# Weight sums of a Strassen-style MLP made during the input projection, silu by tanh, and other buffers for the output projection

## The chip, the cores and the metric

One core of a Trainium2 chip runs the kernel. The metric is the time of one execution on the device in microseconds (us): the median of three runs of the kernel before is 2321.2 us (2319.56 to 2322.18).

The engines are TensorE (PE; its weight loads are listed as PEld), VectorE (DVE), ScalarE (ACT), GpSimd (POOL) and SyncE (SP). Nearly all DMAs of this kernel are issued on SP, a few on POOL. Each engine works through its own list of instructions in order, and an instruction that waits holds up what is behind it in that list.

## The reference

One layer of a streaming encoder over 2048 prompt frames and 64 sample frames, model width 1024, all in float32:

```
a = rmsnorm(x, norm1)
qa, ka, va, qr, kr, vr, gr = split(a @ w_in)      # queries and keys are rotated by position
attn = windowed attention with a sink per head (window of 2 chunks of 64 frames + the own chunk)
ret  = chunkwise retention with a state per head
r    = ret * rsqrt(mean(ret * ret) + EPS) * silu(gr)
h    = x + concat(attn, r) @ w_out
u    = relu(rmsnorm(h, norm2) @ w_up)             # 1024 -> 4096
y    = h + (u * u) @ w_down                       # 4096 -> 1024
out  = rmsnorm(y, norm_f)                         # and new keys, values and retention states
```

Here silu(g) = g / (1 + exp(-g)), which is also 0.5 * g * (1 + tanh(g / 2)). In the kernel g = rs * z, where z is the product before the norm and rs the norm's factor of a row.

## The kernel before

The 2112 tokens are worked in 16 tiles of 128 and one of 64 in the projection, and in NP = 3 parts of PN = 704 columns (two blocks of NB = 352) after it. A product in full precision is made of three matmuls: each operand is split into a high part (ACT, L620) and a low part (DVE, L621), and high x high, high x low and low x high are added up in PSUM.

**The input projection** (0 to about 750 us) goes through the tiles twice: phase `ph` = 0 and 1 each have half of the heads' columns, in three column groups `ci` (384, 512 and 512 columns). `groups` (L549) lists (phase, tile, column group). The loop at L570 starts, at the first group of a tile, the loads of the next tile: `xr` (the input, 512 KB), `rt` (rotation tables) and, in phase 0, `xk` (the input again, for the norm). Then `group` (L516) issues the matmuls of a group and, among them, what `run_ready` finds due of the attention and retention work of earlier tiles. The order of PE and SP in this stage is that order of the code (`manual_schedule`, L553); DVE, ACT and POOL are ordered by the framework's scheduler. The gate `sig` is made of ACT's exp (L352), DVE's add (L353), DVE's reciprocal (L354) and one more DVE operation (L356). `xl`, the low part of the input, is a subtraction on POOL (L154). `hl` (L232) holds the split rotated queries and keys, `pl` (L315) the low part of the transposed softmax weights.

The weights of this stage pass through the pool `wraw` (4 buffers, tag "raw"); it is used for weights at the start of a phase only.

**The output projection** (about 750 to 945 us) is `out_part` (L671): for each part and each of 8 column tiles `d` it loads and splits weights `wo` (L676 to L681) and multiplies with `mhl`, the split mixture, which `load_mix` (L660) loads through `mraw` (3 buffers of its own). `hooks` names the work issued after step d of a part: `norm_part` (L704: two matmuls with ones per block, names `pn` and `nr`, then DVE operations on `nt`), `a_sums` (L713, sums of the activation) and `a_operand` (L728, loading and splitting such a sum to `ah` and `al`).

**The MLP** multiplies blocks of matrices with seven products in place of eight (`ORDER`, `RIGHT`, `LEFT`). Each weight block needs four sums of its quarters: `left_sums` (L650), three on DVE and one on POOL. For the up weights this happens in part 0 (`up_weights`, L778): load two blocks of 512 KB (`up`), make the sums (`su`), use them, and store them to `uscr`; parts 1 and 2 load them from there (`upr`, 256 KB each). `up_pair` (L799) makes one pair of column blocks; there are 16 pairs in a part. For the down weights, `down_sums` (L765) loads two blocks of 512 KB (`dnraw`), makes the sums (`sd`) and stores them to `sscr`, once after every second pair of parts 1 and 2. All these loads go to the 6 buffers of `rawslot` (pool `wr`). From about 1644 us the down projection reads `sscr` (`dr`, split to `wd`), and its matmuls are L971 to L973.

After the input projection its pools are given back (`p1.close()`, L592), and the pools of the later stages lie over the same memory; a buffer laid over an earlier one waits until that one's last user has finished. `side="right"` puts a pool at the other end of the memory.

## Time and profile before

| | |
|---|---|
| median of 3 runs | 2321.2 us (2319.56 to 2322.18) |
| the profiled execution, its own time | 2321.18 us |
| its span in the trace | 2319.4 us |
| PE busy | 97% of the span |
| DVE / ACT / POOL busy | 70% / 48% / 20% |
| memory read / written | 348.28 MB / 135.99 MB |

The page lists busy time of each engine, the granted TensorE clock, DMA queues, the chain of work that ended last, and groups of instructions. A row of a group reads: line, engine, operation, output <- inputs, partitions x elements, count | busy us, mean ns of one | idle time of the engine just before them and what ended it. A row of the timeline reads: start, duration (both us), engine, line, operation, and in brackets the idle time before it and what ended it. A row of stretches reads: from:to and length in us, then busy time and count of PE, PEld, DVE, ACT and POOL, the granted clock (1.00 is full), the mean busy share of the 16 DMA engines (the records of transfers can overlap, so it can come out above 1) and GB/s. A row of DMA issues reads: destination <- source, issuing queue, kind, count, KB each, median us from issue to landing.

In the chain that ended last, PE has 42% of the span, DMA 8% and DVE 6%; the costliest lines are the down projection's L971 to L973.

### The profile page before, as it was taken

To read this page: it belongs to the slowest core of one execution; us is meant where nothing else is said; L and a number is where in the kernel's file an instruction comes from. 1 tells how busy PE (TensorE), PEld (TensorE's weight loads), DVE (VectorE), ACT (ScalarE), POOL (GpSimd) and SP (SyncE) were. 2 spreads that over 40 slices of the span, in tenths; PEclk is the share of its full clock that TensorE was granted. 3 is DMA by queue.
4 is the path that set the end of the run, shared out by engine and by line. 5 is a ranking of instruction groups with operands and counts; after the bars stand their busy time and mean duration, and the time that the engine had idled before them with its cause. 6 is when DMAs were issued, how large, how long until landed. Compare 5 with 4: busy or idle time off the path is not lost.

```text
span 2319.4 us, 35611 instructions
## 1 busy us (share of the span) xinstructions
PE 2243.5 (97%) x13256; PEld 2134.9 (92%) x13256; DVE 1634.6 (70%) x2645; ACT 1109.3 (48%) x1985; POOL 462.9 (20%) x533
## 2 busy tenths in 40 slices
PE   7999999999998999799999999999999999999998
PEld 5888888888886999799999899999999999999998
DVE  6676677666666567887787778777766876677665
ACT  5444454444434433355565556655554444444452
POOL 5444343433333111211000000000000200110012
PEclk9999999999998999899999999999999999999999
DMA  6222223111114778776699999999976776677662
GB/s 191 78 66 70 79 91 116 56 49 47 43 53 143 243 245 288 272 245 232 233 318 345 356 321 334 335 320 302 368 242 235 270 272 243 225 266 275 233 211 78
DMA packets 242734, 486.55 MB, mean 210 GB/s; under 512 B 20560, under 2 KB 126224, under 8 KB 242560
## 3 DMA queue, kind: packets, MB, share of 16 engines
q1 hardware_dynamic: 238592, 474.40, 60.4%
q0 software_dynamic: 3968, 9.87, 1.4%
q8 instruction: 104, 1.70, 0.3%
q14 instruction: 70, 0.57, 0.1%
HBM read 348.28 MB, written 135.99 MB: 209 GB/s over the span
## 4 chain that ended last, share of the span: by engine, by line
PE 42%; DMA 8%; DVE 6%; issue 2%; ACT 1%; SPq 0%; DVEq 0%; POOL 0%; ACTq 0%
PE y L971 10%; PE y L973 9%; PE y L972 9%; DMA up<-in_wup 3%; DMA upr<-uscr 2%; PE b L811 2%; PE b L813 2%; PE b L812 2%; DVE wu L621 2%; PE a L811 1%; PE a L813 1%; PE c L811 1%; PE a L812 1%; PE c L813 1%; PE c L812 1%
## 5 line engine op out<-in xcount | busy, mean ns | idle before, releaser
L973 PE MATMUL y<-vh,wd 128*128 128x352 f32 x1344 | 438.1, 326 | 2.1 <-DVE wd L621 2.1
L971 PE MATMUL y<-vh,wd 128*128 128x352 f32 x1344 | 439.2, 327 | 0.6 <-ACT wd L620 0.6
L972 PE MATMUL y<-vl,wd 128*128 128x352 f32 x1344 | 434.2, 323 | 0.0
L529 PE MATMUL z<-w,xh 128*128 128x512 f32 (+1 forms) x816 | 326.1, 400 | 7.3 <-ACT w L86 7.3
L530 PE MATMUL z<-w,xh 128*128 128x512 f32 (+1 forms) x816 | 310.2, 380 | 1.3 <-DVE w L87 1.3
L620 ACT ACTIVATE wd<-dr 128x1024 fp32r<-128x1024 f32 x168 | 177.2, 1056 | 268.2 <-PE y L973 184.4
L532 PE MATMUL z<-w,xl 128*128 128x512 f32 (+1 forms) x768 | 288.9, 376 | 0.1
L621 DVE TENSOR_TENSOR wd<-dr,wd 128x1024 fp32r<-128x1024 f32 x168 | 208.5, 1244 | 113.3 <-ACT wd L620 110.9
L971 PEld LDWEIGHTS y<-vh,wd 128*128 128x128 f32 x1344 | 253.6, 189 | 0.9 <-ACT wd L620 0.9
L973 PEld LDWEIGHTS y<-vh,wd 128*128 128x128 f32 x1344 | 252.0, 187 | 2.4 <-DVE wd L621 2.4
L972 PEld LDWEIGHTS y<-vl,wd 128*128 128x128 f32 x1344 | 253.1, 188 | 0.0
L811 PE MATMUL b<-ah,wu 128*128 128x352 f32 x576 | 188.2, 328 | 7.9 <-DVE u L822 6.6
L922 POOL TENSOR_TENSOR acc<-acc,sq 128x352 f32<-128x352 f32 x41 | 68.9, 1681 | 605.3 <-ACT sq L918 605.3
L813 PE MATMUL b<-ah,wu 128*128 128x352 f32 x576 | 186.5, 324 | 0.0
L812 PE MATMUL b<-al,wu 128*128 128x352 f32 x576 | 185.9, 323 | 0.0
L529 PEld LDWEIGHTS z<-w,xh 128*128 128x128 f32 x816 | 156.2, 191 | 25.8 <-ACT w L86 7.7
L530 PEld LDWEIGHTS z<-w,xh 128*128 128x128 f32 x816 | 156.2, 191 | 23.0 <-DVE w L87 5.2
L620 ACT ACTIVATE wu<-upr 128x512 fp32r<-128x512 f32 x224 | 134.5, 625 | 88.6 <-DMA upr<-in_wup 53.0
L621 DVE TENSOR_TENSOR wu<-upr,wu 128x512 fp32r<-128x512 f32 x224 | 151.4, 698 | 34.2 <-ACT wu L620 33.4
L532 PEld LDWEIGHTS z<-w,xl 128*128 128x128 f32 x768 | 144.8, 189 | 23.5 <-DVE xl L154 0.4
L621 DVE TENSOR_TENSOR vl<-rv,vh 128x1408 fp32r<-128x1408 f32 x84 | 137.3, 1638 | 36.7 <-ACT vh L620 35.6
L620 ACT ACTIVATE vh<-rv 128x1408 fp32r<-128x1408 f32 x84 | 115.8, 1379 | 48.2 <-DMA rv<-vscr 28.8
(292 smaller groups left out, 5108.4 us busy)
## 6 DMA issues: line engine op xcount, KB each, us to landing
rv<-vscr SPq DMA_DIRECT2D x84, 704.0 KB, 5.7
vscr<-C SPq DMA_DIRECT2D x48, 1056.0 KB, 7.4
dr<-sscr SPq DMA_DIRECT2D x96, 512.0 KB, 4.5
dr<-in_wdn SPq DMA_DIRECT2D x72, 512.0 KB, 4.8
upr<-uscr SPq DMA_DIRECT2D x128, 256.0 KB, 6.7
upr<-in_wup SPq DMA_DIRECT2D x96, 256.0 KB, 6.5
up<-in_wup SPq DMA_DIRECT2D x32, 512.0 KB, 6.0
uscr<-su SPq DMA_DIRECT2D x32, 512.0 KB, 2.9
```

What stands on the lines that cost most here:

```text
L529: nc.tensor.matmul(z[:, :n], xh[:, k], wh, start=k == 0, stop=False)
L530: nc.tensor.matmul(z[:, :n], xh[:, k], wl, start=False, stop=k == NK - 1 and xl is None)
L532: nc.tensor.matmul(z[:, :n], xl[:, k], wh, start=False, stop=k == NK - 1)
L620: nc.scalar.activation(h, x, AF.Copy)
L621: sub(l, x, h.bitcast(F32))
L811: nc.tensor.matmul(o, wh, ah[:, k], start=k == 0 and i in (1, 6, 5), stop=False, skip_group_check=True)
L812: nc.tensor.matmul(o, wh, al[:, k], start=False, stop=False, skip_group_check=True)
L813: nc.tensor.matmul(o, wl, ah[:, k], start=False, stop=k == 3 and i in (2, 4, 3), skip_group_check=True)
L922: nc.gpsimd.tensor_add(self.acc, self.acc, sq)
L971: nc.tensor.matmul(o, wh, vh, start=f == 0, stop=False)
L972: nc.tensor.matmul(o, wh, vl, start=False, stop=False)
L973: nc.tensor.matmul(o, wl, vh, start=False, stop=f == 15)
```

## The change

It has four parts, all in one diff.

1. **Sums.** `sum_unit(u)` makes 64 units, 32 of the up weights and 32 of the down weights. A unit loads two pieces of 256 KB into a buffer `sr`, makes four sums of 128x256 on DVE into `st`, and stores 512 KB to `uscr` or `sscr`. Both buffers come from `wraw`. The projection's loop first stores the unit of the group before, then loads the next one, then starts the tile's own loads. Units run from tile 3 of phase 0 until the weights of phase 1 come, and from the third tile of phase 1 on. `left_sums` and `down_sums` are gone, and part 0 of the up projection loads its seven operands from `uscr` and `wup`, as parts 1 and 2 do.
2. **Gate.** ACT computes tanh(z * rs / 2) in place of the exp; DVE's add and reciprocal are gone; `sig` becomes (tanh + 1) * z. The missing factor rs / 2 goes into the row factor `rr` of the retention output, by way of `ss`, for one more small POOL operation a tile in phase 0.
3. **Pools.** `wr`, `wp` and `wd` go to the right side and `qp` to the left, so that `qp` (the mixture's buffers) lies over `wraw` and the input's first weights. `mraw` is taken from the six `rawslot` buffers, not from three of its own.
4. **Hooks.** `norm_part(0)` and `norm_part(1)` come one step d later, `norm_part(2)` after the second pair of the up projection, not the first.

```
@@ -68,7 +68,7 @@
...
-    nrsc = cp.tile([128, NT], F32, name="nrsc")
+    hrs = cp.tile([128, NT], F32, name="hrs")
...
@@ -165,7 +165,8 @@
             ms = xp.tile([128, 1], F32, name="ms")
             nc.gpsimd.tensor_scalar(ms[:T], ss[:T, t:t + 1], 1.0 / D, EPS, op0=ALU.mult, op1=ALU.add)
             nc.gpsimd.tensor_tensor(rs[:T, t:t + 1], ms[:T], mhalf[:T, 0:1], op=ALU.pow)
-            nc.gpsimd.tensor_scalar(nrsc[:T, t:t + 1], rs[:T, t:t + 1], -1.0, None, op0=ALU.mult)
+            nc.gpsimd.tensor_scalar(hrs[:T, t:t + 1], rs[:T, t:t + 1], 0.5, None, op0=ALU.mult)
+            nc.gpsimd.tensor_scalar(ss[:T, t:t + 1], ms[:T], 4.0 / 128, None, op0=ALU.mult)
...
@@ -347,13 +348,12 @@
...
+
...
         sig = wk.tile([128, 256], F32, name="sig")
-        nc.scalar.activation(sig[:T], gz, AF.Exp, scale=nrsc[:T, t:t + 1])
-        nc.vector.tensor_scalar(sig[:T], sig[:T], 1.0, None, op0=ALU.add)
-        nc.vector.reciprocal(sig[:T], sig[:T])
+        nc.scalar.activation(sig[:T], gz, AF.Tanh, scale=hrs[:T, t:t + 1])
         c.sil = sig
-        nc.vector.scalar_tensor_tensor(sig[:T], gz, rs[:T, t:t + 1], sig[:T], op0=ALU.mult, op1=ALU.mult)
+        nc.vector.scalar_tensor_tensor(sig[:T], sig[:T], 1.0, gz, op0=ALU.add, op1=ALU.mult)
...
@@ -391,7 +391,7 @@
...
-        nc.gpsimd.tensor_scalar(s2[:T], s2[:T], 1.0 / 128, EPS, op0=ALU.mult, op1=ALU.add)
+        nc.gpsimd.tensor_scalar(s2[:T], s2[:T], 128 * EPS, ss[:T, t:t + 1], op0=ALU.add, op1=ALU.mult)
         nc.gpsimd.tensor_tensor(rr[:T], s2[:T], mhalf[:T], op=ALU.pow)
...
@@ -567,7 +567,38 @@
...
+    def sum_unit(u):
+
+
+        w, j, h = u // 32, u % 32 // 2, u % 2
+        r, s = (wraw.tile([128, 4, 256], F32, name=n, tag="raw") for n in ("sr", "st"))
+        if w == 0:
+            c = slice(h * 256, h * 256 + 256)
+            src = [wup[e].rearrange("p (a c) -> p a c", a=2)[:, :, c] for e in (j, j + 16)]
+            dst = uscr[:, j, :, c]
+        else:
+            d, c = j // 4, slice((j % 4 * 2 + h) * 256, (j % 4 * 2 + h) * 256 + 256)
+            src = [wdn[e].rearrange("p (a f) n -> p a (f n)", a=2)[:, :, c] for e in (d, d + 4)]
+            dst = sscr[:, d, :, c]
+        for k in range(2):
+            nc.sync.dma_start(r[:, 2 * k:2 * k + 2], src[k])
+        L11, L12, L21, L22 = (r[:, k] for k in range(4))
+        nc.vector.tensor_add(s[:, 0], L21, L22)
+        nc.vector.tensor_sub(s[:, 2], L11, L21)
+        nc.vector.tensor_sub(s[:, 1], s[:, 0], L11)
+        nc.vector.tensor_sub(s[:, 3], L12, s[:, 1])
+        return lambda: nc.sync.dma_start(dst.rearrange("s p c -> p s c"), s)
+
+    todo = list(range(64))
+    store = None
+    first, change = groups.index((0, 3, 0)), groups.index((0, S - 2, 0))
+
     for i, (ph, t, ci) in enumerate(groups):
+        if store:
+            store()
+            store = None
+        if todo and (first <= i < change or ph == 1 and t > 1):
+            store = sum_unit(todo.pop(0))
...
@@ -585,6 +616,7 @@
...
+    assert not todo and not store
...
@@ -595,11 +627,11 @@
...
-    wr = ctx.enter_context(pool(name="wr", bufs=6))
+    qp = ctx.enter_context(pool(name="qp", bufs=16))
     ar = ctx.enter_context(pool(name="ar", bufs=2))
-    qp = ctx.enter_context(pool(name="qp", bufs=16, side="right"))
+    wr = ctx.enter_context(pool(name="wr", bufs=6, side="right"))
     upper = ExitStack()
-    wp = upper.enter_context(pool(name="wp", bufs=9))
+    wp = upper.enter_context(pool(name="wp", bufs=9, side="right"))
...
@@ -647,13 +679,6 @@
...
-    def left_sums(sA, sB, L11, L12, L21, L22):
-
-        add(sA[:, 0], L21, L22)
-        nc.gpsimd.tensor_sub(sB[:, 0], L11, L21)
-        sub(sA[:, 1], sA[:, 0], L11)
-        sub(sB[:, 1], L12, sA[:, 1])
-
...
@@ -661,7 +686,7 @@
...
         for f in range(8):
-            raw = op.tile([128, PN], F32, name="mraw", bufs=3)
+            raw = rawslot("mraw")[:, :PN]
             nc.sync.dma_start(raw, mscr[f, :, n0:n0 + PN])
             t = qp.tile([128, 2, PN], F32R, name="mhl", tag="q")
             split(t[:, 0], t[:, 1], raw)
@@ -748,12 +773,11 @@
...
         accs[0] = out_part(0, mixes[0], {})
         accs[1] = out_part(1, mixes[1], {
-            0: [lambda: norm_part(0, accs[0])],
+            1: [lambda: norm_part(0, accs[0])],
             2: [later(a_sums, 0, 0, opslot), lambda: put(mixes, 2, load_mix, 2)],
             3: [later(a_sums, 0, 1, opslot)], 4: [later(a_sums, 0, 2, opslot)], 5: [later(a_sums, 0, 3, opslot)]})
         accs[2] = out_part(2, mixes[2], {
-            0: [lambda: norm_part(1, accs[1])],
-            1: [lambda: put(A, (0, ORDER[0]), a_operand, 0, ORDER[0])],
+            1: [lambda: norm_part(1, accs[1]), lambda: put(A, (0, ORDER[0]), a_operand, 0, ORDER[0])],
             2: [lambda: put(A, (0, ORDER[1]), a_operand, 0, ORDER[1]), later(a_sums, 1, 0, opslot)],
             3: [lambda: put(A, (0, ORDER[2]), a_operand, 0, ORDER[2]), later(a_sums, 1, 1, opslot)],
             4: [lambda: put(A, (0, ORDER[3]), a_operand, 0, ORDER[3]), later(a_sums, 1, 2, opslot)],
@@ -762,30 +786,7 @@
...
-    def down_sums(u):
-        d, fq = u // 4, u % 4
-        c = slice(fq * 512, fq * 512 + 512)
-        rw = []
-        for e in (d, d + 4):
-            r = rawslot("dnraw").rearrange("p (a n) -> p a n", a=2)
-            nc.sync.dma_start(r, wdn[e].rearrange("p (a f) n -> p a (f n)", a=2)[:, :, c])
-            rw.append(r)
-        sA, sB = (rawslot("sd").rearrange("p (a n) -> p a n", a=2) for _ in range(2))
-        left_sums(sA, sB, rw[0][:, 0], rw[0][:, 1], rw[1][:, 0], rw[1][:, 1])
-        nc.sync.dma_start(sscr[0:2, d, :, c].rearrange("a p n -> p a n"), sA)
-        nc.sync.dma_start(sscr[2:4, d, :, c].rearrange("a p n -> p a n"), sB)
-
-    def up_weights(p, j):
-        if p == 0:
-            r0, r1 = rawslot("up0"), rawslot("up1")
-            nc.sync.dma_start(r0, wup[j])
-            nc.sync.dma_start(r1, wup[j + 16])
-            L11, L12, L21, L22 = r0[:, :512], r0[:, 512:], r1[:, :512], r1[:, 512:]
-            sA, sB = (rawslot("su").rearrange("p (a n) -> p a n", a=2) for _ in range(2))
-            left_sums(sA, sB, L11, L12, L21, L22)
-            nc.sync.dma_start(uscr[0:2, j].rearrange("a p n -> p a n"), sA)
-            nc.sync.dma_start(uscr[2:4, j].rearrange("a p n -> p a n"), sB)
-            return {1: L11, 6: sA[:, 1], 5: sA[:, 0], 7: sB[:, 0], 2: L12, 4: L22, 3: sB[:, 1]}
+    def up_weights(j):
         src = {}
         for n, i in enumerate(ORDER):
             if n % 2 == 0:
@@ -797,7 +798,7 @@
...
     def up_pair(p, j, after):
-        src = up_weights(p, j)
+        src = up_weights(j)
         a, b, c = psum("a"), psum("b"), zp.tile([128, 512], F32, name="c", tag="z")
         bank = {1: a, 2: a, 6: b, 7: b, 4: b, 5: c, 3: c}
         C = up.tile([128, 8, NB], F32, name="C", bufs=2)
@@ -842,16 +843,14 @@
...
             for j in range(16):
                 up_pair(p, j, after)
-                if (p, j) == (0, 0):
+                if (p, j) == (0, 1):
                     norm_part(2, accs[2])
                 if p == 1 and j in (2, 4, 6, 8):
                     a_sums(2, j // 2 - 1, arslot)
-                if p > 0 and j % 2:
-                    down_sums(8 * (p - 1) + j // 2)
     upper.close()
-    wd = ctx.enter_context(pool(name="wd", bufs=4))
+    wd = ctx.enter_context(pool(name="wd", bufs=4, side="right"))
     xp2 = ctx.enter_context(pool(name="xp2", bufs=1, side="right"))
...
```

On SP, in the input projection in phase 0, where one tile's DMAs are issued (`xr`, `rt`, `xk` as above). Before, these three rows are a whole tile:

```order
L142 DMA xr<-in_xt 128x8x128
L160 DMA rt<-in_rot 128x384
L163 DMA xk<-in_xtok 128x1024
L142 DMA xr<-in_xt 128x8x128
L160 DMA rt<-in_rot 128x384
```

And after the change (`sr` is a unit's load, `st` its sums):

```order
L142 DMA xr<-in_xt 128x8x128
L160 DMA rt<-in_rot 128x384
L163 DMA xk<-in_xtok 128x1024
L590 DMA uscr<-st 128x4x256
L584 DMA sr<-in_wup 128x2x256 x2
L590 DMA uscr<-st 128x4x256
L584 DMA sr<-in_wup 128x2x256 x2
L590 DMA uscr<-st 128x4x256
L584 DMA sr<-in_wup 128x2x256 x2
L142 DMA xr<-in_xt 128x8x128
```

Three units stand between the loads of two tiles, and each store, which waits for its sums, stands ahead of the next unit's loads.

On DVE, in the input projection, from the softmax weights `p` of a tile to the queries and keys `hl`, before:

```order
L300 TENSOR_SCALAR p<-p,sm 128x192 x4
L376 TENSOR_TENSOR sd<-pss,dm 128x256
L353 TENSOR_SCALAR sig<-sig 128x256
L354 RECIPROCAL sig<-sig 128x256
L315 TENSOR_TENSOR pl<-pt,ph 128x512 x2
L356 SCALAR_TENSOR_TENSOR sig<-z,rs,sig 128x256
```

And after the change, from `mix`, which stands just ahead of `hl`, to `rqT`, and from `p` to `pl`:

```order
L334 TENSOR_TENSOR mix<-po,ob 64x256 x2
L586 TENSOR_TENSOR st<-sr 128x256
L233 TENSOR_TENSOR hl<-zr,hl 128x6x64
L587 TENSOR_TENSOR st<-sr 128x256
L588 TENSOR_TENSOR st<-st,sr 128x256
L589 TENSOR_TENSOR st<-sr,st 128x256
```

```order
L287 SCALAR_TENSOR_TENSOR ngm<-mx,nsk 128x2
L588 TENSOR_TENSOR st<-st,sr 128x256
L589 TENSOR_TENSOR st<-sr,st 128x256
L366 TENSOR_TENSOR rqT<-ptr,qd 128x256
L295 TENSOR_TENSOR sm<-sm,es 128x4
L296 RECIPROCAL sm<-sm 128x4
L301 TENSOR_SCALAR p<-p,sm 128x192 x4
L376 TENSOR_TENSOR sd<-pss,dm 128x256
L586 TENSOR_TENSOR st<-sr 128x256
L587 TENSOR_TENSOR st<-sr 128x256
L356 SCALAR_TENSOR_TENSOR sig<-sig,z 128x256
L588 TENSOR_TENSOR st<-st,sr 128x256
```

A tile has three units' sums: one around `hl`, one that ends ahead of `rqT`, and one after `sd`, where the gate's add and reciprocal stood; behind the last row stand `pl` and the unit's fourth sum.

On DVE, at the end of the input projection, around the last tile (64 frames, `zz`, `hl 64x6x64`), before:

```order
L621 TENSOR_TENSOR wo<-woraw,wo 128x512 x4
L353 TENSOR_SCALAR sig<-sig 64x256
L621 TENSOR_TENSOR wo<-woraw,wo 128x512 x2
L404 SCALAR_TENSOR_TENSOR st_8007<-sts_7988,pst 128x128
L404 SCALAR_TENSOR_TENSOR st_8010<-sts_7990,pst 128x128
L232 TENSOR_TENSOR hl<-zr,hl 64x6x64
L354 RECIPROCAL sig<-sig 64x256
L333 TENSOR_TENSOR mix<-po,ob 64x256 x2
L621 TENSOR_TENSOR wo<-woraw,wo 128x512 x3
L356 SCALAR_TENSOR_TENSOR sig<-zz,rs,sig 64x256
L285 TENSOR_REDUCE mx<-s 128x2
```

And after the change:

```order
L653 TENSOR_TENSOR mhl<-mraw,mhl 128x704 x3
L356 SCALAR_TENSOR_TENSOR sig<-sig,zz 64x256
L653 TENSOR_TENSOR mhl<-mraw,mhl 128x704 x2
L233 TENSOR_TENSOR hl<-zr,hl 64x6x64
L404 SCALAR_TENSOR_TENSOR st_8532<-sts_8513,pst 128x128
L404 SCALAR_TENSOR_TENSOR st_8535<-sts_8515,pst 128x128
L334 TENSOR_TENSOR mix<-po,ob 64x256 x2
L653 TENSOR_TENSOR mhl<-mraw,mhl 128x704 x2
L409 SCALAR_TENSOR_TENSOR ro<-pr,rr,sig 64x128 x2
L653 TENSOR_TENSOR mhl<-mraw,mhl 128x704 x3
L286 TENSOR_REDUCE mx<-s 128x2
```

The splits of the mixture (`mhl`, 16 of them ahead of `mx`, of which six stand above these rows) have come between the last tile's operations; the splits of the first weights (`wo`) have gone behind them.

## The prediction

> **What bounds the kernel now.** I read the page's engine totals first, then busy time by stretch, then PE's waits in the stretches that fall short.
>
> ```profile
> span 2319.4 us, 35611 instructions
> PE 2243.5 (97%) x13256; PEld 2134.9 (92%) x13256; DVE 1634.6 (70%) x2645; ACT 1109.3 (48%) x1985; POOL 462.9 (20%) x533
> ...
> core 0: us, PE busy (x) PEld busy (x) DVE busy (x) ACT busy (x) POOL busy (x), PEclk, DMA share, GB/s
> 410.00:720.00 310.00, 310.00 (x1771) 273.00 (x1770) 206.04 (x465) 128.31 (x401) 112.66 (x153) 1.00 0.18 52
> 757.00:928.00 171.00, 166.25 (x1030) 165.67 (x1030) 113.65 (x167) 63.26 (x91) 32.43 (x18) 1.00 0.78 259
> 928.00:990.00 62.00, 48.08 (x258) 46.26 (x257) 52.24 (x72) 20.46 (x31) 15.11 (x6) 0.86 0.76 269
> 990.00:1160.00 170.00, 167.58 (x1021) 165.43 (x1021) 135.42 (x221) 92.83 (x136) 22.04 (x13) 1.00 0.69 238
> 1276.00:1340.00 64.00, 56.14 (x326) 53.67 (x325) 44.86 (x74) 34.06 (x47) 3.10 (x2) 0.97 1.03 355
> 1606.00:1650.00 44.00, 38.77 (x226) 37.60 (x225) 32.48 (x45) 26.27 (x31) 1.63 (x1) 0.96 0.97 331
> 1650.00:2290.00 640.00, 640.00 (x3926) 640.00 (x3926) 435.62 (x455) 303.08 (x309) 66.43 (x39) 1.00 0.71 248
> ```
>
> PE is busy 97% of the span: only its gaps can be won, since the change touches no matmul of a product. A full stretch (1650 to 2290) gives the pace, 3926/640 = 6.13 matmuls per us. The others, by their counts at that pace, are short by: 757 to 928, 171 - 1030/6.13 = 3; 928 to 990, 62 - 258/6.13 = 20 (granted clock 0.86); 990 to 1160, 3.5; 1276 to 1340, 64 - 326/6.13 = 11 (DMA share 1.03, the highest); 1606 to 1650, 7. From 410 to 720, in the input projection, PE is busy 310 of 310 us: there nothing can be won, only lost.
>
> ```profile
> PE c L813 <- DVE wu L621: 4.2, 1, 4.2
> PE pn__10156 L630 <- DVE nr L628: 3.5, 1, 3.5
> PE a L811 <- DVE nt L633: 2.9, 1, 2.9
> PE pn__9424 L630 <- DVE nr L628: 2.8, 1, 2.8
> PE pn__8785 L630 <- DVE nr L628: 1.9, 1, 1.9
> ...
> PE a L811 <- ACT wu L620: 5.4, 3, 2.6
> ```
>
> These are PE's waits (total, times, longest) from 757 to 990 and, below the gap, from 1270 to 1345. The first five are DVE being late where the next part begins. The last follows a split of weights, which comes after the weights' loads.
>
> **The sums that leave the MLP.**
>
> ```profile
> L655 DVE TENSOR_TENSOR su<-up,su 128x512 f32<-128x512 f32 x16 | 21.1, 1321 | 0.0
> L654 DVE TENSOR_TENSOR sd<-sd,dnraw 128x512 f32<-128x512 f32 x16 | 11.0, 685 | 0.2
> ...
> dnraw<-in_wdn SPq DMA_DIRECT2D x32, 512.0 KB, 8.1
> sscr<-sd SPq DMA_DIRECT2D x32, 512.0 KB, 7.7
> ```
>
> - Parts 1 and 2 of the up projection lose, in every second pair, two loads and two stores of 512 KB, 2 MB of a pair of pairs, landing in 8.1 and 7.7 us. The remaining loads no longer queue behind them on SP. Of the 11 us at 1276 to 1340 I return 9 (the wait for the split holds 5.4 of them, and PE at the lower clock that follows idle time comes with it: granted 0.97), of the 7 at 1606 to 1650 I return 4 (the rest is the first weights of the next stage). Bounds 0 and 18: **-13**.
> - Part 0 loses 16 sets of DVE sums, about 1.32 + 0.69 + 0.69 = 2.7 us of each pair. At 990 to 1160 I return 2 of 3.5 (bounds 0 and 3.5). Its bytes from memory stay about equal: seven loads of 256 KB in place of 1 MB in and 1 MB out.
> - At 928 to 990 the sums of the first pair go (the wait for wu, 4.2 us), and norm 2 stands one pair later. But DVE still has 52 of 62 us there, with the activation's operand splits, which nothing removes, and the waits for nr (3.5) and nt (2.9) move with the norm. I return 7 of 20: **-7** (bounds 0 and 16).
> - Norms 0 and 1 stand one weight tile later: the waits 1.9 and 2.8 are covered by at least the next tile's 48 matmuls, 8 us: **-3**.
>
> Sum of the gains: -13 - 2 - 7 - 3 = **-25**, bounds 0 and -40.
>
> **The sums that enter the projection.** There are 64 units, three to a tile in steady running, on 21 tiles. SP runs a loop: wait for a unit's sums, store it, load the next unit; DVE does that unit's sums at three fixed places of the tile (before and after `hl`, among `ngm`, and after `sd`).
>
> ```profile
> 521.30 0.75 DVE L195 SCALAR_TENSOR_TENSOR rot<-z,rs,rt 128x512 f32<-128x512 f32 x1 [2.32 <-PE z L532]
> 528.66 0.43 DVE L376 TENSOR_TENSOR sd<-pss,dm 128x256 f32<-128x256 f32 x1 [0.74 <-PE pss L373]
> 529.12 2.37 POOL L154 TENSOR_TENSOR xl<-xr,xh 128x1024 fp32r<-128x1024 f32 x1 [4.21 <-DVE sd L376]
> 529.96 1.98 DVE L353 TENSOR_SCALAR sig<-sig 128x256 f32<-128x256 f32 x1 [0.87 <-ACT sig L352]
> 531.52 0.55 SPq L142 DMA_DIRECT2D xr<-in_xt  x1
> 533.63 1.22 DVE L315 TENSOR_TENSOR pl<-pt,ph 128x512 fp32r<-128x512 f32 x2
> 538.75 0.56 DVE L232 TENSOR_TENSOR hl<-zr,hl 128x384 fp32r<-128x384 f32 x1 [0.62 <-ACT hl L230]
> 540.88 0.46 PE L246 MATMUL pq<-idr,hl 128*128 128x128 f32 x4
> 542.31 0.75 DVE L195 SCALAR_TENSOR_TENSOR rot<-z,rs,rt 128x512 f32<-128x512 f32 x1 [2.99 <-PE z L532]
> ...
> L354 DVE RECIPROCAL sig<-sig 128x256 f32<-128x256 f32 x32 | 56.1, 1753 | 1.0
> L353 DVE TENSOR_SCALAR sig<-sig 128x256 f32<-128x256 f32 x32 | 53.1, 1660 | 31.3 <-ACT sig L352 31.3
> L154 DVE TENSOR_TENSOR xh<-xr,xh 128x256 fp32r<-128x256 f32 x2 | 0.9, 426 | 2.3 <-ACT xh L153 2.3
> ...
> xr<-in_xt SPq DMA_DIRECT2D x31, 512.0 KB, 4.2
> uscr<-su SPq DMA_DIRECT2D x32, 512.0 KB, 2.9
> ```
>
> - DVE's work: tanh removes 53 + 56 = 109 us. The 256 sums of 128x256 are not in the trace; the nearest rows are 0.43 us (128x256) and half of 0.69 (128x512), so 88 to 110 us. Even, and DVE has 104 of 310 us free there. ACT's tanh takes the place of its exp, one for one.
> - Where they stand: after `sd` the sums take the place of L353 and L354, 3.7 us that stood ahead of `pl`; four sums and `sig` take about 2. So a unit that comes 1.5 us late there costs nothing. `hl` ends at 539.3, and PE asks for it at 540.9: 1.5 us of cover. Beyond this cover every late sum stalls PE.
> - The loop: the period of a tile is 542.31 - 521.30 = 21.0 us. One turn is the store's issue (0.55, xr's issue row) and the loads' landing, 4.2 by xr (as many bytes): 4.75. Bounds: 4.2 if the store adds nothing, 2.9 + 4.2 = 7.1 if the loads move only after the store. I take 4.75 since the two go in opposite directions. DVE's part: 12 sums x 0.385 = 4.6 and, between a unit's first and last sum, `hl` 0.56, `ngm` about 0.3, `sig` about 0.5, `pl` 1.22: 7.2 us. Loop: 3 x 4.75 + 7.2 = 21.45, or 0.45 over the tile's period: x 21 tiles = **+9**. With 4.2 it is 19.8, free; with 7.1 it is 28.5, +158. The rt load, queued on SP between the turns, waits for DVE's rotation and lies inside one of them: part of the turn's uncertainty.
>
> The Trainium skill, "DMA: Bandwidth & Descriptors", section "Anatomy of one DMA — SWDGE (gpsimd) path", puts a transfer at about 2.0 us and its bytes at 436 GB/s: 4.4 us for the turn's 1 MB, an estimate, by which the loop would be 20.4, free, and the sum 9 lower; these transfers are issued from SP and no run here shows the fit for them.
>
> **The transition at 720 to 757.** The output projection's `mhl` splits now stand between the last tile's operations, where wo's splits stood.
>
> ```profile
> 742.64 0.54 DVE L285 TENSOR_REDUCE mx<-s 128x2 f32<-128x384 f32 x1
> 749.88 2.71 PE L690 MATMUL y<-mhl,wo 128*128 128x352 f32 x8 [1.21 <-ACT mhl L620]
> L621 DVE TENSOR_TENSOR wo<-woraw,wo 128x512 fp32r<-128x512 f32 x48 | 35.4, 747 | 7.7 <-ACT wo L620 7.4
> L621 DVE TENSOR_TENSOR mhl<-mraw,mhl 128x704 fp32r<-128x704 f32 x24 | 21.8, 923 | 19.9 <-ACT mhl L620 19.8
> ```
>
> Before `mx` stand 16 splits of 0.92 = 14.8 us in place of nine of 0.75 and two reciprocals of 1.75 = 10.2 us: the last tile's softmax comes about 4.6 us later, and what is queued behind it (`ngm`, p, pt, po, and then y) with it. Behind y the mix is then ready, but wo's splits are not. **+5** (bounds -3, if the mix that is ready earlier returns the slow first y, and +10).
>
> **Sum.** -25 + 9 + 5 = -11. The profiled execution took 2321.18 us (span 2319.4 and 1.8 around it), which is the median of 2321.2: **2310**.
>
> **Rivals.**
> - *More is returned and the loop is free.* For it: a turn of 4.2 us makes the loop shorter than the tile; the wait of 4.2 for wu goes whole. Against: two transfers share the queues. -25 - 6 more at 928 to 990, +5, 0: **2295**, 18%.
> - *The loop is late* (other side). The mechanism is the turn store, load, sum on SP; its price is 3 x 21 = 63 times each us of a turn over 4.6. Gains less transition are 20, so it decides at 21.95 - 7.2 = 14.75, a turn of 4.92 us; above 4.99 the kernel is slower by over 0.2%. For it: the store's 2.9 us stand ahead of the loads on the same queues; xr's 512 KB join them. Against: DMA share 0.18 from 410 to 720. At 5.3 us the loop is 23.1, +44: **2345**, 14%.
> - *The sums after `sd` wait for POOL's `xl`.* L353, a cheap operation, takes 1.98 us beside xl's 2.37 above. A first sum that starts at about 551.5 meets xl until 552.5, 1 us a tile in the loop, +21: **2331**, 10%. The Trainium skill, "SBUF — State Buffer", section "SBUF: two separate sides", says that a VectorE operation with two SBUF inputs and a GpSimd one that reads SBUF hold a shared port in turn, each for its whole length; all 256 sums have two SBUF inputs. L353's 1.98 beside 2.37 agrees.
> - *The waits only move*: norms and operand splits fill DVE at the new places, and 928 to 990 and the norms return nothing (-25 + 10): **2320**, 12%.
>
> **How the numbers follow.** The forecast, 2310 (2303 to 2316), has 46%. A measurement of this kernel tells about 0.2%, 4.6 us, from no change. Faster: 46 + 18 + 3 of the last rival = 67%; same: its other 9%; slower: 14 + 10 = 24%. The range from 2286 to 2340 takes in the second case with 9 us below it, and the third slow case; it leaves out the late loop above a turn of 5.2 us (about 10%) and some 4% below.
>
> **What would show it.** The loop: `st` sums idle on their loads from 410 to 720, and PE's 310 of 310 becoming less; by the forecast 6 to 7 us less, by a late loop over 30. The MLP: the stretch of part 1 that lost 11 losing 2, dnraw's rows gone and upr's landing under 6.5 us. The norms: nr's waits of 1.9 and 2.8 gone, one of about 3 left in the up projection. The transition: y first at about 755 less what the projection shifted. I am wrong if the up projection keeps its gaps with the 2 MB gone, or if a turn's landing is far from 4.75 us.

## The result, and the profile after

The changed kernel takes 2385.08 us (median of 4 runs, 2379.33 to 2386.79) beside 2320.94 us before in the same comparison: a ratio of 1.0276, 95% interval 1.026 to 1.0292. It is slower by 64 us, outside the range of the prediction and on the side of its third case.

First the page of the changed kernel, and its stretches of time (columns as before: from:to and length, busy time and count of PE, PEld, DVE, ACT, POOL, granted clock, DMA share, GB/s). From 850 us on it runs some 99 us behind the kernel before, so the last four rows stand for the rows 928 to 990, 990 to 1160, 1276 to 1340 and 1606 to 1650 of the prediction.

```profile
span 2384.2 us, 35986 instructions
PE 2240.7 (94%) x13256; PEld 2125.1 (89%) x13256; DVE 1565.1 (66%) x2737; ACT 1116.3 (47%) x1985; POOL 418.8 (18%) x518
...
410.00:720.00 310.00, 267.26 (x1454) 229.64 (x1453) 174.31 (x485) 108.06 (x336) 96.64 (x130) 0.96 0.57 144
850.00:1027.00 177.00, 170.84 (x1055) 170.84 (x1056) 105.83 (x159) 56.78 (x86) 32.17 (x18) 0.97 0.70 237
1027.00:1089.00 62.00, 42.75 (x233) 40.99 (x232) 49.42 (x65) 22.06 (x31) 7.97 (x5) 0.81 0.84 296
1089.00:1259.00 170.00, 170.00 (x1064) 170.00 (x1063) 116.76 (x195) 98.48 (x141) 0.00 (x0) 1.00 0.70 229
1375.00:1439.00 64.00, 64.00 (x402) 64.00 (x401) 42.91 (x72) 36.22 (x55) 0.00 (x0) 1.00 0.77 261
1705.00:1749.00 44.00, 40.91 (x239) 40.33 (x237) 28.56 (x30) 25.98 (x25) 0.00 (x0) 0.92 0.94 339
```

The MLP did what it should but for its first pairs: the stretch that lost 11 us is full (64 of 64, DMA share 0.77 for 1.03), and 990 to 1160's successor is full too; 928 to 990's successor has 233 matmuls in place of 258, at a granted clock of 0.81 for 0.86. The input projection did not: PE, busy for 310 of 310 us before, has 267, and 1454 matmuls in place of 1771. DVE is busy for 174 us there, for 206 before; for each matmul that is about the same (0.120 us for 0.116), so this is not too much work; it waits.

PE's waits of the changed kernel, from 410 to 720 us and, below the gap, from 815 to 870 and from 1035 to 1110:

```profile
PE pss L373 <- ACT rkT L367: 21.8, 9, 4.6
PE pq L247 <- DVE hl L233: 18.7, 8, 4.3
...
PE y L715 <- ACT wo L652: 6.4, 1, 6.4
...
PE a L812 <- ACT pc L817: 9.7, 1, 9.7
```

`pq` waits for `hl`, and `pss` for `rqT` and `rkT`: the two places ahead of which a unit's sums stand in DVE's order. One tile of DVE's and SP's timeline shows why they are late (start, duration, instruction, idle time before and what ended it). Of the last four rows, two are DMA issues of the whole run and two are DVE's waits for these loads from 60 to 850 us (total, times, longest):

```profile
590.13 0.42 DVE L586 TENSOR_TENSOR st<-sr 128x256 f32<-128x256 f32 x1 [3.87 <-DMA sr<-in_wdn]
591.33 0.42 DVE L589 TENSOR_TENSOR st<-sr,st 128x256 f32<-128x256 f32 x1
591.67 0.42 DVE L366 TENSOR_TENSOR rqT<-ptr,qd 128x256 f32<-128x256 f32 x1
598.62 0.42 DVE L586 TENSOR_TENSOR st<-sr 128x256 f32<-128x256 f32 x1 [3.83 <-DMA sr<-in_wdn]
608.83 0.43 DVE L586 TENSOR_TENSOR st<-sr 128x256 f32<-128x256 f32 x1 [4.87 <-DMA sr<-in_wdn]
609.51 0.55 DVE L233 TENSOR_TENSOR hl<-zr,hl 128x384 fp32r<-128x384 f32 x1
618.84 0.42 DVE L586 TENSOR_TENSOR st<-sr 128x256 f32<-128x256 f32 x1 [2.95 <-DMA sr<-in_wdn]
...
591.78 0.37 SPq L590 DMA_DIRECT2D sscr<-st  x1
592.25 1.50 SPq L584 DMA_DIRECT2D sr<-in_wdn  x2
...
sr<-in_wup SPq DMA_DIRECT2D x64, 256.0 KB, 4.2
sr<-in_wdn SPq DMA_DIRECT2D x64, 256.0 KB, 5.4
...
DVE st L586 <- DMA sr<-in_wdn: 103.4, 31, 6.0
DVE st L586 <- DMA sr<-in_wup: 71.1, 30, 3.7
```

A unit's sums end at 591.75, the store is issued at 591.78, the two loads from 592.25 to 593.75, and the next sums start when the data land, at 598.62: a turn of 6.9 us. The next turns, read in the same way, take 7.6 and 8.0. DVE stands idle for 3 to 5 us ahead of each unit, with `rqT` or `hl` behind it, and the tile takes 618.84 - 590.13 = 28.7 us, not 21.0.

This tile is one of the slow ones. From the store's issue to the start of the next sums, the 62 turns other than the last and the one across the change of weights take 4.8 to 6.9 us with the up weights (phase 0, 5.7 in the mean) and 5.0 to 8.9 us with the down weights (phase 1, 6.9 in the mean).

In phase 0 a second thing holds the sums, POOL's `xl`:

```profile
274.05 2.38 POOL L154 TENSOR_TENSOR xl<-xr,xh 128x1024 fp32r<-128x1024 f32 x1
274.08 2.62 DVE L586 TENSOR_TENSOR st<-sr 128x256 f32<-128x256 f32 x1 [2.79 <-DMA sr<-in_wup]
```

Eleven of the 256 sums, ten of them in phase 0, stand beside `xl` in this way and take 1.3 to 2.6 us in place of 0.42: 20 us of DVE's time in all.

To divide the time of each run I read three marks off its profiled execution: the start of the output projection's first matmul `y`, the start of the up projection's first matmul `a`, and the end of the span. PE's order in the projection is the same in all of them.

| run | first y at | y to first a | first a to the end |
|---|---|---|---|
| before | 749.9 | 195.0 | 1374.5 |
| changed kernel | 856.2 | 187.7 | 1340.4 |
| e1, loads ahead of the store | 813.5 | 187.6 | 1340.2 |
| e2, before with tanh alone | 741.7 | 196.9 | 1378.6 |
| e3, changed, sums back in the MLP | 752.3 | 188.6 | 1367.6 |
| e6, double units | 802.8 | 187.8 | 1340.4 |
| e7, e1 with rt on POOL's queue | 805.3 | 187.1 | 1339.7 |
| e8, e7 with 8 buffers in wp | 796.3 | 189.5 | 1343.6 |
| e9, e7 with the old norm places | 803.9 | 189.2 | 1336.0 |
| e10, e8 with xr on POOL's queue | 815.5 | 188.8 | 1341.7 |
| e11, e10 with the sums one group later | 824.4 | 190.1 | 1342.1 |
| e12, sums without loads | 793.9 | 187.3 | 1339.9 |
| e13, down sums alone in the projection, 8 buffers in wp | 770.9 | 189.6 | 1351.1 |
| e14, sums without waits for transfers | 785.0 | 187.4 | 1341.2 |
| e15, e3 with the down sums spread, 8 buffers in wp | 740.1 | 189.1 | 1363.2 |
| e16, e15 with the old norm places | 742.1 | 189.9 | 1354.9 |
| e17, e2 with the down sums spread | 736.4 | 196.9 | 1369.9 |

The changed kernel loses 106 us up to the first y and gains 7 + 34 after it: 65 us in all, the difference of the spans. Each row is a single execution: e2 and e17 are the same program up to the first y, and their rows differ by 5.3 us there; e2's is the slowest of its ten, 2318.99 us.

### The profile page after: what moved, and what is told of

Read it like the earlier page. It is cut to its first block, busy times and chain, and to the rows that moved or that the text cites. A ratio compares the mean times of both kernels' runs of the same rounds, so it can differ in the third digit from the quotient of the medians.

```text
span 2384.2 us, 35986 instructions
## 1 busy us (share of the span) xinstructions
PE 2240.7 (94%) x13256; PEld 2125.1 (89%) x13256; DVE 1565.1 (66%) x2737; ACT 1116.3 (47%) x1985; POOL 418.8 (18%) x518
## 4 chain that ended last, share of the span: by engine, by line
PE 54%; DMA 2%; DVE 2%; issue 1%; ACT 0%; DVEq 0%; POOL 0%; SPq 0%; ACTq 0%
PE y L971 9%; PE y L972 9%; PE y L970 9%; PE b L814 4%; PE b L813 4%; PE b L812 4%; PE a L812 3%; PE a L813 3%; PE a L814 3%; PE c L814 3%; PE c L813 3%; PE c L812 3%; DMA hscr<-xres 1%; DMA xres<-in_xt 1%; DMA rr<-ascr 0%
## 5 line engine op out<-in xcount | busy, mean ns | idle before, releaser
L529 PE MATMUL z<-w,xh 128*128 128x512 f32 (+1 forms) x816 | 330.3, 405 | 8.2 <-ACT w L86 8.2
L530 PE MATMUL z<-w,xh 128*128 128x512 f32 (+1 forms) x816 | 313.3, 384 | 1.5 <-DVE w L87 1.5
L653 DVE TENSOR_TENSOR wu<-upr,wu 128x512 fp32r<-128x512 f32 x336 | 232.8, 698 | 81.8 <-ACT wu L652 64.9
L652 ACT ACTIVATE wu<-upr 128x512 fp32r<-128x512 f32 x336 | 209.8, 628 | 149.1 <-PE b L814 78.5
L529 PEld LDWEIGHTS z<-w,xh 128*128 128x128 f32 x816 | 158.6, 194 | 27.1 <-ACT w L86 8.5
L530 PEld LDWEIGHTS z<-w,xh 128*128 128x128 f32 x816 | 158.7, 194 | 21.8 <-DVE w L87 3.6
L586 DVE TENSOR_TENSOR st<-sr 128x256 f32<-128x256 f32 x64 | 39.0, 610 | 174.6 <-DMA sr<-in_wdn 103.4
```

What stands on the lines that cost most here:

```text
L529: nc.tensor.matmul(z[:, :n], xh[:, k], wh, start=k == 0, stop=False)
L530: nc.tensor.matmul(z[:, :n], xh[:, k], wl, start=False, stop=k == NK - 1 and xl is None)
L652: nc.scalar.activation(h, x, AF.Copy)
L653: sub(l, x, h.bitcast(F32))
```

## The experiments

Times are medians; ratios are to the kernel before in the same comparison, with their 95% interval.

**e1: the order on SP.**

```
-        if store:
-            store()
-            store = None
+        ready_store, store = store, None
         if todo and (first <= i < change or ph == 1 and t > 1):
             store = sum_unit(todo.pop(0))
+        if ready_store:
+            ready_store()
```

> The changed kernel with two statements exchanged: at a group's start the next unit's loads are issued ahead of the store of the unit before, so that they no longer stand behind a wait for sums. Same transfers, same sums. Theory A (the turn sums, store, loads, landing of about 7 us, three times a tile, sets the tile's period): the period falls from 28 us to 21 and about 95 us return, 2285 to 2300 us. Theory B (the sums themselves, in DVE's order ahead of hl and rqT and beside POOL's xl, delay PE whatever their data does): above 2350. Theory C (the transfers are slow and crowd each other): part of it returns, 2310 to 2350.

2343.45 us, ratio 1.0106 (1.0087 to 1.0125): 43 us return in the first y, less than theory A said and in theory C's interval. Its SP timeline shows what stood in the way next:

```profile
569.50 0.55 SPq L142 DMA_DIRECT2D xr<-in_xt  x1
581.16 0.35 SPq L160 DMA_DIRECT2D rt<-in_rot  x1
581.61 1.20 SPq L584 DMA_DIRECT2D sr<-in_wdn  x2
582.86 0.59 SPq L590 DMA_DIRECT2D sscr<-st  x1
583.55 2.02 SPq L584 DMA_DIRECT2D sr<-in_wdn  x2
```

SP issues nothing from 570 to 581: `rt` waits for DVE's rotation of the tile, and the next units' loads stand behind it.

**e6: half as many turns of twice the size.**

```
+        rs_ = [wraw.tile([128, 2, 512], F32, name=n, tag="raw") for n in ("sr0", "sr1")]
+        s = [wraw.tile([128, 2, 512], F32, name=n, tag="raw") for n in ("st0", "st1")]
...
+            turn += 1
+            if turn % 2:
```

> The changed kernel with 32 units of twice the size (rows of 2 KB, sums of 128x512), one every second group, the store still ahead of the next loads: same bytes, half the turns. Theory A: 1.5 turns of about 8.5 us and 7 us of sums are 20 us, less than a tile's 21, so most of the loss returns, 2290 to 2315. Theory B: the same DVE work in larger pieces, 2370 or more. Theory C: longer rows help the transfers only, 2330 to 2370.

2333.28 us, ratio 1.006 (1.0037 to 1.0082): 52 us return, with the store still ahead of the loads. This is in theory C's interval, not in A's: the longer rows came together with half the turns, and this run does not tell the two apart. Where sums waited for their loads, a turn took 7.7 to 10.4 us with the up weights and 9.2 to 11.7 with the down weights, not A's 8.5. That fewer turns help about as much as a better order fits the turn; half of the loss stays, so the turn is not all.

**e7, e8 and e9: rt on POOL's queue, then a buffer fewer in wp, or the norms put back.**

```
-        nc.sync.dma_start(rt[:T], rot[t0:t0 + T])
+        (nc.gpsimd if (ph, t) in aux_pool else nc.sync).dma_start(rt[:T], rot[t0:t0 + T])
...
-    wp = upper.enter_context(pool(name="wp", bufs=9, side="right"))
+    wp = upper.enter_context(pool(name="wp", bufs=8, side="right"))
...
-            1: [lambda: norm_part(0, accs[0])],
+            0: [lambda: norm_part(0, accs[0])],
...
-                if (p, j) == (0, 1):
+                if (p, j) == (0, 0):
                     norm_part(2, accs[2])
```

> e1 (loads ahead of the store) with the rotation tables rt loaded by POOL's queue, not SP's. In e1's trace SP stands 11 us a tile on rt's load, which waits for DVE's rotation, and the loads of three units are crowded into the rest of the tile. Theory D (this wait on SP is what e1 left): PE's stretches from 60 to 720 us fill up, about 50 us return, 2285 to 2300 us. Rival (loads that land in 5.5 to 6 us, or DVE's own order, hold the sums): no better than 2330.

> e7 with 8 buffers in wp, not 9, so that none lies over the memory of the last mixture. Theory (the first split of wo waits 5 to 6 us for the last mixture's store, because the ninth buffer lies over it): PE's wait for wo of 6 to 8 us at the start of the output projection goes, 4 to 7 us less than e7. Rival (the loads of woraw end as late, or one buffer less costs elsewhere): within 2 us of e7, or slower.

> e7 with the three norms where they were before the change. The prediction's term: the later place gains 3 us and part of 7 at the first pairs, so this run is 3 to 6 us slower than e7. By the changed kernel's trace (25 us lost around the first pairs, 22 us before the change; a wait of 9.7 us for the first pair's eviction): the same as e7 within 3 us, or up to 5 us faster.

e7: 2333.72 us, 1.0068 (1.0053 to 1.0083), only 10 us below e1, as the rival had it. Theory D fails as a whole: the queue has another such place. e8: 2329.47, 1.0041 (1.0025 to 1.0056), 4 us below e7, at the edge of the noise; the wait for `wo` went from 6.7 to 4.6 us in the profiles, so it did not go. e9: 2333.47, 1.007 (1.0055 to 1.0085), equal to e7: here the norms' places do not matter as a whole. By the table the later places save 2 us ahead of the first `a` and cost 4 behind it. e7's SP shows the other place, a wait of 9.5 us behind the store:

```profile
578.93 0.36 SPq L592 DMA_DIRECT2D sscr<-st  x1
588.82 0.55 SPq L142 DMA_DIRECT2D xr<-in_xt  x1
589.46 1.27 SPq L586 DMA_DIRECT2D sr<-in_wdn  x2
```

`xr` has one buffer, which POOL's `xl` gives back.

**e10 and e11: xr on POOL's queue too; sums one group later in the code.**

```
-            nc.sync.dma_start(xr[:, a[0]:a[1], :T], xt[:, a[0]:a[1], t0:t0 + T])
+            (nc.sync if first or t in (NT - 1, 0, 1, 2) else nc.gpsimd).dma_start(xr[:, a[0]:a[1], :T], xt[:, a[0]:a[1], t0:t0 + T])
...
+        if todo and (first <= i < change - 1 or ph == 1 and t > 1):
+            sums = sum_unit(todo.pop(0))
+        if ready_store:
+            ready_store()
+        if ready_sums:
+            store = ready_sums()
```

> e8 with the input xr loaded by POOL's queue too: SP then carries only xk, the units' loads and their stores. In e7's trace SP stands 9 us a tile on xr's load, which waits for POOL's xl. If SP's foreign waits are what is left, the projection fills up: 2329 to 2280-2295. If what is left is that DVE's order has the three units' sums within some 10 us of a tile, so that each waits for a load that can be issued only when the unit two before it is done, little returns: 2320 to 2335.

> e10 with a unit's sums written one group later in the code, behind the next unit's loads. Same dependencies; DVE's order still has the sums in a cluster. If the time between a load's issue and its sums' place decides: 10 us or more below e10. If the cluster decides: within 10 us of e10.

2350.7 us, 1.0145 (1.0117 to 1.0173), and 2354.91, 1.0162 (1.0143 to 1.0181). e10 is slower than e8 by 21 us, more than either theory allowed; e11 is within 10 us of e10, so a later place in the code is no cure. SP is free of foreign waits now, and with them went what had spread the units over the tiles. In DVE's order of e10 some 20 sums, five units, stand between one `xl` and the next, 12 in e7, so that phase 0 has used up its units by 235 us. In phase 0 its tiles with some 20 sums take 25 to 31 us from `xl` to `xl`, and the later ones, without sums, 21.0. These later tiles too load `rt` and `xr` from POOL's queue, so those issues alone cost nothing there; the crowded sums go with the 21 us, and no run tested them alone.

**e12 and e14: the sums without their transfers.** e12 takes a resident weight tile as input; in e14 the input is the tile's own split input, and the stores send a resident tile. In both, the weights of the MLP are not the reference's.

```
-        for k in range(2):
-            nc.sync.dma_start(r[:, 2 * k:2 * k + 2], src[k])
-        L11, L12, L21, L22 = (r[:, k] for k in range(4))
+        r = xs[ph, t][0].rearrange("p k n -> p (k n)").bitcast(F32)
+        res = ws[ph, 1][0].rearrange("p a b n -> p (a b n)").bitcast(F32)
+        L11, L12, L21, L22 = (r[:, k * 256:k * 256 + 256] for k in range(4))
```

> The changed kernel without the units' loads: the sums take a resident weight tile of the projection as their input (so the MLP's weights are not the reference's), the stores stay. It tells the data's arrival from DVE's work. Theory (DVE stands waiting for the loads, with hl, rqT and pl behind the sums): the projection fills up but for a few us, 2285 to 2300. Theory B (256 more operations in DVE's order and beside POOL's xl delay PE themselves): above 2340.

> The changed kernel without the units' loads, and with stores that send a resident weight tile, so that no sum waits for a transfer and no transfer for a sum (the MLP's weights are then not the reference's). The 768 instructions fewer or more on DVE are the same 256 sums, of the tile's own split input; DVE's order has a tile's twelve sums behind sd, beside POOL's xl. If waits for transfers (loads, or stores held up in SP's order) are the whole loss: PE loses at most 10 us from 100 us on in the projection, 2280 to 2295. If DVE's work and its port shared with POOL delay PE themselves, as the p operation's 3.1 us beside xl in the run without loads suggests: 20 to 40 us stay, 2305 to 2325.

e12: 2327.9 us, 1.0041 (1.0025 to 1.0058). Neither theory: the sums still waited, for buffers that a store held up on SP had not given back (11 times, 21.5 us in all, from 410 to 720 us). e14: 2317.43, 0.9995 (0.9981 to 1.0008). That is in its second interval. No sum waits for a transfer any more, and the first y comes at 785.0, 71 us earlier than in the changed kernel and 33 later than in e3, which has no sums there. So of 104 us, **71 go with the waits for transfers, and 33 stay without them**. How far this holds for the changed kernel is open: in e14 a tile's sums stand together behind `sd`, and they wait for ACT's split of the input (13 times, 17.9 us in all, from 60 to 720 us), which the changed kernel's do not. One part of the 33 is visible in most tiles: twenty sums of e14 stand beside `xl` and take 2.2 to 2.9 us each. First e12, then e14, each with POOL's `xl` and the DVE operation beside it:

```profile
573.30 2.35 POOL L154 TENSOR_TENSOR xl<-xr,xh 128x1024 fp32r<-128x1024 f32 x1 [4.21 <-ACT xh L153]
573.34 3.11 DVE L301 TENSOR_SCALAR p<-p,sm 128x192 f32<-128x192 f32 x4
```

```profile
574.59 2.62 POOL L154 TENSOR_TENSOR xl<-xr,xh 128x1024 fp32r<-128x1024 f32 x1 [4.22 <-DVE sd L376]
574.89 2.61 DVE L587 TENSOR_TENSOR st<-xh 128x256 f32<-128x256 f32 x1
577.42 0.41 DVE L586 TENSOR_TENSOR st<-xh 128x256 f32<-128x256 f32 x1
```

The four `p` operations take 3.11 us here and 1.01 us apart from `xl`; a sum of 0.41 us takes 2.61. The rest of the 33 us lies in small waits, most of them in phase 0 (1464 matmuls from 60 to 340 us, 1590 in e3; from 410 to 720 us 1711 and 1767) and was not taken further apart.

**e2, e3 and e13: parts of the change.** e2 is the kernel before with the lines of the gate alone; e3 the changed kernel with `left_sums`, `down_sums` and the old `up_weights` back and `todo = []`; e13 has only the 32 units of the down weights in the projection, in every second group, the sums of the up weights back in part 0, and 8 buffers in wp:

```
-    todo = list(range(64))
+    todo = list(range(32, 64))
+    turn = 0
...
+            turn += 1
+            if turn % 2:
+                store = sum_unit(todo.pop(0))
```

> The kernel before with the gate by tanh alone. All theories: PE is full there and DVE has a third of its time free, so within 0.2% of the kernel before, 2316 to 2326. If the removed 109 us of DVE were on a path that the profile hides, below 2310.

> The changed kernel with the weight sums where they were, in the up projection; pools, hooks and gate stay changed. By the prediction's terms: +5 for the transition, -3 for the norms, a few us less at the first pairs: 2318 to 2324. By the trace of the changed kernel (wo's first split waits for the last mixture's store, 5 us; the second pair waits 10 us for the first pair's eviction): about 2325 to 2340.

> The changed kernel with only the 32 units of the down weights in the projection, one every second group; the up weights' sums are in part 0 of the up projection as before, and wp has 8 buffers. Loop by the turn's measured 7 us: 1.5 x 7 + 3.6 = 14 us of a tile's 21, so nearly free; the second and third part of the up projection keep their gain of about 15 us over e3 (2309.5) and wo's first split its 5: 2288 to 2302. If the loss of the projection goes by the number of sums and not by the turn: 2325 or more.

e2: 2309.75 us, 0.9953 (0.9934 to 0.9973), a gain of some 9 us, at the edge of the second case (below 2310) and outside the one that all theories had. e3: 2309.5, 0.9965 (0.9947 to 0.9983): below both expectations, the first by about the gate's gain. e13: 2315.9, 0.9992 (0.9979 to 1.0004), between its two cases; its first y, at 770.9, is some 30 us behind those of e15 and e16, which have no sums in the projection and 8 buffers in wp like e13. So half of the sums at half the rate still cost nearly a third of the 104 us.

**e15, e16 and e17: what the trace points to.** The gap at 1276 to 1340 us came where the activation sums of the third part and the down sums stood between the same pairs. e15 is e3 with 8 buffers in wp and

```
+    DOWN_AT = [(0, j) for j in (5, 7, 9, 11, 13, 15)] + [(1, j) for j in (9, 11, 13, 15)] \
+        + [(2, j) for j in (1, 3, 5, 7, 9, 11)]
...
-                if p > 0 and j % 2:
-                    down_sums(8 * (p - 1) + j // 2)
+                if (p, j) in DOWN_AT:
+                    down_sums(DOWN_AT.index((p, j)))
```

e16 puts the three norms back to their old places, e17 is e2 with this list.

> The kernel of e3 (sums in the MLP, gate by tanh, changed pools and hooks) with 8 buffers in wp and the 16 sets of down sums moved off the pairs in which the third part's activation sums run: 6 in part 0 from pair 5 on, 4 in part 1 from pair 9 on, 6 in part 2. The gap of some 10 us where both stood together in part 1 should close and wo's first split come 5 us earlier: 2294 to 2303, the fastest so far. If part 0 has no room (DVE is busy 135 of 170 us there): 2303 to 2312.

> e15 with the three norms at their old places. The prediction gave the later places a gain of 3 us and part of 7; then this run is 3 to 6 us slower than e15. e15's own count (32 us lost from 900 to 1000 us, about 20 in the kernel before) speaks for the opposite: 3 to 10 us faster than e15, 2288 to 2295.

> The kernel before with the gate by tanh and the down sums spread as in e15: old pools, old hooks. If pools and hooks together bring nothing (e3 and e2 were equal at 2309.5 and 2309.75): the spread alone takes about 10 us off e2, 2297 to 2303. If the pools bring about 5 us and the hooks cost as much: within 3 us of e15 on either side.

e15: 2297.95 us, 0.9913 (0.9892 to 0.9934). **e16: 2287.89, 0.9862 (0.9838 to 0.9886), the fastest of all.** e17: 2303.25, 0.9928 (0.9906 to 0.9951). The stretch that lost 11 us is full in e17, which has nothing else of the change but the gate; in e2 PE is busy for 56.48 us of it:

```profile
1276.00:1340.00 64.00, 64.00 (x396) 64.00 (x395) 47.69 (x82) 35.46 (x53) 2.91 (x2) 1.00 0.89 307
```

PE's waits around the first pairs, first e15, then e16:

```profile
PE a L845 <- ACT pc L850: 15.1, 1, 15.1
```

```profile
PE a L846 <- ACT pc L851: 3.4, 1, 3.4
```

In e15, with norm 2 after the second pair and the weight sums in the MLP, the first pair's eviction `pc` comes 15.1 us late; with the norm at its old place, 3.4. Between e17 and e16 lie the pools and the eight buffers: 15 us. In their profiles, 16 us apart, 7.0 are the output projection (196.9 to 189.9) and 15.0 the stretch after it, less 5.7 that the transition costs.

## Why the prediction was wrong, step by step

- **The sums that leave the MLP** (-13 and -2, and the 4.2 of the first wu inside the -7). Right, and a little small: e3 to the changed kernel is 27.2 us in the stretch from the first a on (1367.6 to 1340.4). The gap of 11 us closed. The first pairs themselves, from which the -7 was to come, got no better: 62 - 233/6.13 = 24 us short, where 928 to 990 was 20, as the fourth rival had it.
- **The loop** (+9). This is the step that failed, in its size: "One turn is the store's issue (0.55, xr's issue row) and the loads' landing, 4.2 by xr (as many bytes): 4.75." The turn measured 5.7 us in the mean with the up weights and 6.9 with the down weights, near the upper bound of 7.1. Its parts: the two loads' issue took 1.50 us, where the prediction had no time for it; they landed 4.2 us after their issue with the up weights, just as xr's had, and 5.4 with the down weights, in rows of the same length; why these took longer stays open. The Trainium skill's fit ("DMA: Bandwidth & Descriptors", section "Anatomy of one DMA — SWDGE (gpsimd) path"), by which the prediction estimated 4.4 us for the turn, is further off still; it is stated for DMAs issued from GpSimd, and these are not. With the measured turns the prediction's own form comes out right in sum: 3 x 5.7 + 7.2 is 3.3 us over the tile's 21.0, on 11 tiles, and 3 x 6.9 + 7.2 is 6.9 over it, on 10: about 105, an estimate, beside 103.9 from e3 to the changed kernel. In the tile shown it holds by its parts: 6.9 + 7.6 + 8.0 = 22.5, and 6.2 of DVE, 28.7. The rt load, which the prediction counted to the turn's uncertainty, is a place of its own: taken off SP it returned 10 us (e1 to e7). The direction was the third case, with its point at 4.92; the price of that case was taken for 5.3; 57 of the 62 turns took more than 4.99.
- **DVE's work: "Even".** Counted right (0.120 us for each matmul, 0.116 before), but its place was not free: e14 keeps 33 us without any wait for a transfer, of which the waits that only its own sums have (17.9 us of DVE's time) may be a part. The third rival, sums that wait for POOL's `xl`, came true beside the late loop: it had 1 us a tile, 21 us; the changed kernel has 20 us of it on DVE, nearly all in phase 0 and with 0.9 to 2.2 us a time. What of this reached PE was not measured. The Trainium skill ("SBUF — State Buffer", section "SBUF: two separate sides") has the rule of one holder at a time for the shared port, and the rows of e12, e14 and the changed kernel agree with it.
- **The gate: nothing gained.** Wrong by 9 us (e2). The prediction said that nothing can be won from 410 to 720; the gain lies elsewhere. e2's count from 340 to 410, at the change of weights, is 382 matmuls and was 350; that accounts for about 5 us. The profiled execution of e2 is its slowest; e17's, with the same projection, has 1600 matmuls from 60 to 340 us where the kernel before has 1579, some 3 us more. Which wait the gate removed was not taken apart.
- **The transition** (+5). e2 to e3 is 10.6 us in the first y, with the 5 us of doubt between single executions. The +5 also counts the gate's two reciprocals, 3.5 us, which e2 has already lost; without them its form gives about 8. The cause named (mhl's splits ahead of `mx`) is there: `pss` waits 3.4 us for them in e15. The other part was overlooked: behind y "the mix is then ready, but wo's splits are not" had no price. In e7 and e8, one buffer less in wp moved the first y by 9 us, the median by 4; with that buffer gone, the first y of e15 and e16 is only 4 to 6 us behind e17's.
- **The norms** (-3, and part of -7). Norms 0 and 1: the two waits are gone with the later places, but in e16 the output projection takes 189.9 us with the old places too, so most of the gain of 7 us there is the pools' (e17 to e16), and about 2 the norms' (e9 to e7). Norm 2: a cost, not a gain, where the MLP still makes its sums (e15 to e16, 10 us), and by the median nothing where it does not (e7 and e9).

The ends of the range came from the terms' own bounds, except the loop's: its upper end of 7.1 us for a turn was worked out, priced at +158, and then left out of the range as unlikely, though the queue's order is exactly what that end describes and the down weights' turns came close to it.

## What to carry to other kernels

Work moved into a stage where an engine has a third of its time free still costs time if each piece waits for a load that the same in-order queue issues only after the piece before it: count the turn (issue of the store, issue of the loads, landing behind the store) and the places of the pieces in the engine's order, not the busy time. Put loads ahead of stores that wait, and look for every other wait of that queue, since each hides behind the one removed; but where such waits had spread the work over time, look what order the engines get once the last is gone (e10). Before moving work far, look whether two bursts merely coincide: spreading the down sums over other pairs (16 sets, no other change beside the gate) took some 6 us (e2 to e17, with intervals that touch), and with the changed pools and eight buffers in wp 22 (e2 to e16).

## What the runs showed of the hardware

- Two loads of 256 KB in rows of 1 KB took 1.50 us to issue on SP, the store of 512 KB before them 0.37, and xr, one load of 512 KB in rows of 512 bytes, 0.55 in the kernel before.
- Loads of 256 KB in rows of 1 KB landed 4.2 us after their issue from the up weights and 5.4 us from the down weights (medians of 64 each, changed kernel).
- A DVE operation beside POOL's subtraction ends shortly after that one: at 577.50 us where `xl` ends at 577.21 (e14), and a sum takes 2.61 us there, 0.41 alone; four `p` operations take 3.11 us beside it and 1.01 apart (e12). In the changed kernel eleven sums were held so.
